# Gates by one ScalarE instruction: Silu for the pool, conv and LayerNorm gates, Tanh with the addition in the eviction for the attention and merge gates

## The chip, the cores and the metric

One core of a Trainium2 chip runs the whole program. The metric is the device time of one execution in microseconds (us), where less is better. The kernel before took 921.75 us in the median of three runs (921.71, 921.75 and 926.39). The profiled execution, from which all rows here come, took 925.56 us. Names in rows: PE is the matmul engine and PEld its weight loads, DVE is VectorE, ACT is ScalarE, POOL is GpSimd, SP is SyncE. "L790" is line 790 of the kernel.

## The reference, cut to what matters

One layer of a hybrid decoder: 1024 prompt tokens and 64 sample tokens (8 sequences of 8) of width 1024, all in fp32. `W` is 512.

```python
h = rmsnorm(x, g_pre)
proj = h @ w_in                                   # 1024 x (7*512 + 3*1024)
p_in, p_gate, c_val, c_glu, c_gate, q, x_gate = [proj[..., i * W:(i + 1) * W] for i in range(7)]
merge_logits = proj[..., 7 * W:].reshape(B, S, 3, D_MODEL)
a = pool_mix(pool_ext, pos0, pool_w, pool_scale) * jax.nn.silu(p_gate)
u = c_val * jax.nn.sigmoid(c_glu)
cv = jax.nn.silu(layernorm(causal_dwconv(conv_ext, conv_w, conv_b), conv_ln_g, conv_ln_b))
bconv = cv * jax.nn.silu(c_gate)
...                                               # o: 4-head attention of q into 256 memory rows
cattn = o * jax.nn.silu(x_gate)
br = jnp.einsum('bsnw,nwd->bsnd', jnp.stack([a, bconv, cattn], axis=2), w_branch)
merged = jnp.sum(jax.nn.sigmoid(merge_logits) * br, axis=2)
x_new = x + rmsnorm(merged @ w_out, g_post)
```

So there are three families of Silu gates on the projections (`p_gate`, `c_gate`, `x_gate`), one Silu after the LayerNorm ("swish"), one sigmoid on `c_glu`, and three sigmoid gates of width 1024 at the merge.

## The kernel before, in words

**Layout.** Tensors lie with channels on the 128 partitions and tokens along the free dimension: 1024 prompt tokens in two halves of 512 (`HALF`), then 64 sample tokens, 1088 in all (`T`). A channel block is a tile `q` of 128x1088 fp32.

**Products.** An fp32 operand is split into two fp16 parts by `hilo`: ACT writes the rounded value (L75), and the rest is written by a subtraction. With a scale of 1.0 that is a TENSOR_TENSOR (L77), on DVE, or on POOL if the caller says so; with any other scale it is a SCALAR_TENSOR_TENSOR on DVE (L79), whatever the caller says. Three matmuls (`mm3`, L85, L88, L89) make one product.

**`pair`.** The input projection goes by pairs of 128-column blocks of `w_in`. One pair is a Strassen-like scheme of 7 products, called stages. Weights come by SP's queue into `raw` tiles; ACT negates some (L498); four DMAs that add at the destination, all issued by POOL (L499, L505, L506, L507), make the sums of weight blocks; `hilo` splits each into a `ws` tile (L75 and L79). ACT (L513) and DVE (L466, `post`) evict the PSUM tiles `pm`: three of the four output blocks of 128x512 end in SBUF, and the fourth, (1, 0), is handed to the caller in PSUM. The caller gives a function `block` for the four blocks and `smp` for the 128x64 sample columns.

**The gates.** `sig_pair` applies a sigmoid to each block (`logistic`, L658): ACT's Sigmoid (L664), or, where `near_exp` is set, ACT's Tanh (L661) and a DVE TENSOR_SCALAR (L662) that makes 0.5*t + 0.5 of it; Tanh is used where the neighbours are exponentials. `silu_pair` (L772) does the same and then multiplies by the projection itself: on POOL for the three blocks that are in SBUF (L790), on DVE from PSUM for block (1, 0) (L788) and the samples (L795). It is called for the attention gate (with `near_exp`), the pool gate and the conv gate (without). The LayerNorm swish takes ACT's Sigmoid (L1093), a DVE TENSOR_SCALAR (L1094) and a POOL multiplication (L1095).

**Attention.** `head` (from L835) multiplies the attention's output in PSUM by the gate tile (L867), splits it and so makes the input `X[2]` of merge 2. The softmax is L824, L827 (Exp), L829 and L832.

**`merge`.** For each of the three branches, eight blocks of gates by `sig_pair`, and for each block the branch projection in three pieces of tokens (364, 364, 360 columns in PSUM tiles `pb`). `ev` (L1155) multiplies piece and gate in one SCALAR_TENSOR_TENSOR, and a DMA issued by POOL (L1161) or DVE (L1157) adds the branches into `M`.

**Out projection.** `pair_of` does `M @ w_out` by the same scheme with M as the stationary side: POOL makes sums of blocks of M into `sr` tiles (L594), `spl` splits them by `hilo` with scale 1.0, and `samples_split` does so for the 64 sample columns, with the subtraction on POOL. DMAs issued by POOL (L1217, `wo_add`) make the sums of `w_out`'s blocks, which are split into `BO`.

**Order.** The sections run in the order conv_pair(0), attn_pair(0), attn_pair(2), conv_pair(2) with the samples' attention, merge(2), pool_pair(0), pool_pair(2), merge(0), cgate_pair(0), cgate_pair(2), merge(1), out projection. A planner hands out stages with side work between: the 120 conv taps of L715 (128x1024 on DVE each) at rates by section, and jobs (softmax, pool mixing, LayerNorm). A scheduler then orders each engine's instructions by a model of their times; the taps are pinned. Every engine runs its list strictly in order, and tiles come from rings of fixed size.

## Time and profile before

| | |
|---|---|
| median of three runs | 921.75 us |
| profiled execution | 925.56 us |
| its span, first to last instruction | 923.8 us |
| mean granted TensorE clock | 0.965 |
| busy: PE, DVE, ACT, POOL | 859.6, 715.1, 465.2, 360.3 us |
| share of the span: PE, DVE, ACT, POOL | 93%, 77%, 50%, 39% |

Times in rows are us unless marked ns. A row of the timeline has start, duration, engine, line, operation, output and input tile, the number of instructions joined, and in brackets how long the engine had stood idle and whose result ended that. A row of a group has the count, the busy time and the mean ns of one, and after the second bar the idle time ahead of them. A row of the table by stages has the stretch, its length, busy time and instruction count of PE, PEld, DVE, ACT and POOL, the granted clock, the DMA share and GB/s.

### The profile page before, as it was taken

How to read it: one execution, taken by the hardware profiler on the slowest of the kernel's cores; microseconds unless marked ns; L12 is line 12 of the kernel's file. 1: busy time of each engine (PE TensorE's matmuls, PEld its weight loads, DVE VectorE, ACT ScalarE, POOL GpSimd, SP SyncE). 2: the span in 40 equal slices, each digit the busy share in tenths (PEclk: the TensorE clock that was granted, in tenths of full speed). 3: DMA queues.
4: the chain of work that ended last, by engine and by line, in shares of the span. 5: the costliest groups of instructions: out<-in, count | busy, mean ns of one | idle time of the engine just before them, and what ended most of it. 6: DMA issues, size and time to landing. Idle time of an engine off the chain costs nothing.

```text
span 923.8 us, 15244 instructions
## 1 busy us (share of the span) xinstructions
PE 859.6 (93%) x5765; PEld 461.0 (50%) x5765; DVE 715.1 (77%) x1119; ACT 465.2 (50%) x990; POOL 360.3 (39%) x392
## 2 busy tenths in 40 slices
PE   5879999999999889999998989999999999988986
PEld 3325455554555545555444445565545555545432
DVE  4697599999967699999988978458565544678876
ACT  8766547554753733323444544356345434745541
POOL 1354152444343361311443775525355212366500
PEclk8869999999999899999999999999999999998998
DMA  8634742424466224334444336444654658472132
GB/s 300 158 65 144 210 97 56 82 68 113 106 224 176 92 39 102 82 80 92 93 95 92 80 86 123 113 110 97 139 117 105 138 122 251 101 158 60 69 126 91
DMA packets 101541, 107.43 MB, mean 116 GB/s; under 512 B 5486, under 2 KB 72036, under 8 KB 101452
## 3 DMA queue, kind: packets, MB, share of 16 engines
q1 hardware_dynamic: 82748, 68.24, 23.5%
q0 software_dynamic: 18720, 38.22, 23.1%
q8 instruction: 45, 0.74, 0.3%
q14 instruction: 28, 0.23, 0.1%
HBM read 62.37 MB, written 6.33 MB: 74 GB/s over the span
## 4 chain that ended last, share of the span: by engine, by line
PE 37%; DVE 15%; issue 5%; ACT 3%; POOL 3%; DMA 3%; DVEq 0%; ACTq 0%; POOLq 0%
PE pm L85 8%; PE pm L89 8%; PE pm L88 8%; DVE q L715 6%; PE pb L85 4%; PE pb L89 4%; PE pb L88 4%; DVE ws L79 3%; DMA raw<-raw 2%; DVE ws L77 1%; POOL sr L594 1%; ACT ws L75 1%; DVE q L1272 1%; DVE q L1265 1%; DVE q L1155 1%
## 5 line engine op out<-in xcount | busy, mean ns | idle before, releaser
L85 PE MATMUL pm<-BO,ws 128*128 128x512 f16 x836 | 319.9, 385 | 17.8 <-ACT h L513 3.7
L89 PE MATMUL pm<-BO,ws 128*128 128x512 f16 x836 | 320.8, 384 | 3.1 <-DVE ws L77 2.8
L88 PE MATMUL pm<-BO,ws 128*128 128x512 f16 x836 | 321.1, 384 | 1.1 <-DVE BO L77 0.6
L79 DVE SCALAR_TENSOR_TENSOR ws<-raw,ws 128x512 f16<-128x512 f32 x228 | 192.9, 863 | 61.2 <-ACT ws L75 59.5
L88 PEld LDWEIGHTS <-ws 128*128 128x128 f16 x1548 | 149.1, 99 | 134.8 <-issue 27.7
L89 PEld LDWEIGHTS <-ws 128*128 128x128 f16 x1548 | 149.3, 99 | 125.0 <-issue 8.0
L85 PEld LDWEIGHTS <-ws 128*128 128x128 f16 x1548 | 148.7, 99 | 117.7 <-issue 9.5
L75 ACT ACTIVATE ws<-raw 128x512 f16<-128x512 f32 x228 | 138.1, 627 | 119.5 <-PE pm L89 57.0
L715 DVE SCALAR_TENSOR_TENSOR q<-q,cw,q 128x1024 f32<-128x1024 f32 x120 | 166.9, 1399 | 4.3 <-ACT q L712 4.0
L85 PE MATMUL pb<-q,ws 128*128 128x364 f16 (+1 forms) x288 | 92.2, 323 | 2.1 <-DVE q L1155 2.1
L89 PE MATMUL pb<-q,ws 128*128 128x364 f16 (+1 forms) x288 | 93.0, 323 | 0.0
L88 PE MATMUL pb<-q,ws 128*128 128x364 f16 (+1 forms) x288 | 92.9, 323 | 0.0
L499 POOL DMA_DIRECT2D raw<-raw x25 | 21.8, 872 | 150.3 <-ACT raw L498 134.1
L513 ACT ACTIVATE h<-pm 128x512 f32<-128x512 f32 x75 | 44.0, 588 | 50.8 <-PE pm L89 47.2
L1155 DVE SCALAR_TENSOR_TENSOR q<-pb,q 128x364 f32<-128x364 f32 (+1 forms) x72 | 37.1, 528 | 30.0 <-PE pb L89 24.4
L466 DVE SCALAR_TENSOR_TENSOR q<-pm,h 128x512 f32<-128x512 f32 x51 | 34.9, 684 | 21.3 <-PE pm L89 13.3
L507 POOL DMA_DIRECT2D raw<-raw x25 | 22.1, 885 | 68.5 <-issue 24.3
L75 ACT ACTIVATE q<-q 128x1024 f16<-128x1024 f32 (+2 forms) x37 | 35.5, 971 | 26.5 <-DVE q L867 12.6
L506 POOL DMA_DIRECT2D raw<-raw x25 | 21.6, 864 | 64.6 <-DVE ws L79 24.7
L498 ACT ACTIVATE raw<-raw 128x512 f32<-128x512 f32 x50 | 31.0, 626 | 30.7 <-DVE ws L79 29.9
L85 PE MATMUL pm<-BS,ws 128*128 128x64 f16 x416 | 43.3, 193 | 1.2 <-DVE q L466 1.2
L664 ACT ACTIVATE q<-q 128x512 f32<-128x512 f32 x36 | 22.6, 627 | 41.7 <-DVE q L466 41.2
(245 smaller groups left out, 1335.1 us busy)
## 6 DMA issues: line engine op xcount, KB each, us to landing
raw<-in_w_in SPq DMA_DIRECT2D x104, 256.0 KB, 2.9
raw<-raw POOLq DMA_DIRECT2D x104, 256.0 KB, 3.2
q<-in_x_prompt SPq DMA_DIRECT2D x16, 512.0 KB, 9.1
q<-q POOLq DMA_DIRECT2D x14, 544.0 KB, 5.5
raw<-in_w_branch SPq DMA_DIRECT2D x24, 256.0 KB, 3.9
q<-in_w_mem_kv SPq DMA_DIRECT2D x8, 512.0 KB, 6.7
q<-in_cache_mem_k SPq DMA_DIRECT2D x8, 512.0 KB, 3.4
q<-in_cache_mem_v SPq DMA_DIRECT2D x8, 512.0 KB, 7.3
```

What stands on the lines that cost most here:

```text
L75: nc.scalar.activation(hi, src, AF.Copy, scale=scale)
L79: nc.vector.scalar_tensor_tensor(lo, src, scale, hi, ALU.mult, ALU.subtract)
L85: ins = nc.tensor.matmul(out, wh, xh, start=start and j == 0, stop=False, skip_group_check=partial)
L88: nc.tensor.matmul(out, wh, xl, start=False, stop=False, skip_group_check=partial)
L89: nc.tensor.matmul(out, wl, xh, start=False, stop=stop and j == n - 1, skip_group_check=partial)
L466: nc.vector.scalar_tensor_tensor(dst, ps, sc, base, ALU.mult, ALU.add)
L498: nc.scalar.activation(A(1, kh), A(1, kh), AF.Copy, scale=-1.0)
L507: nc.gpsimd.dma_start(out=A(0, 1), in_=A(0, 0), accum_op=ALU.add)
L513: nc.scalar.activation(v[name], ps, AF.Copy, scale=sc)
L664: nc.scalar.activation(dst, src, AF.Sigmoid, scale=scale)
L715: ins = nc.vector.scalar_tensor_tensor(acc, src, wj, acc, ALU.mult, ALU.add)
L1155: nc.vector.scalar_tensor_tensor(g, p, 1.0 / WS, g, ALU.mult, ALU.mult)
```

## The change

It replaces four ways of making a gate.

- Pool and conv gates: one ACT instruction, Silu, in place of Sigmoid and a product.
- Attention gate: Tanh of half the argument on ACT, then one DVE SCALAR_TENSOR_TENSOR `(t + 1) * x`. The tile then holds the gate without its factor, which is kept under the key "unit" (0.5, or 0.5/16 for the block out of PSUM), and `head` puts it in.
- LayerNorm swish: one ACT Silu with the LayerNorm's gain and bias as scale and bias.
- Merge gates: Tanh of half the argument in place of Sigmoid, and the eviction computes `(g + 1) * p` in place of `(p / 16) * g`. `M` so holds 32 times its value, and its splits take the factor `MS = 0.5 / WS`: they no longer have the scale 1.0, and the subtraction becomes a SCALAR_TENSOR_TENSOR on DVE, for the samples' columns too, where it was on POOL.

`logistic` stays for conv_pair(2) alone, whose gate keeps Tanh and the TENSOR_SCALAR.

```diff
@@ spl, in pair_of
-                hilo(y, w[:, 0, k], w[:, 1, k])
+                hilo(y, w[:, 0, k], w[:, 1, k], MS)
@@
-    def logistic(dst, src, scale, near_exp):
-        if near_exp:
-            nc.scalar.activation(dst, src, AF.Tanh, scale=0.5 * scale)
-            nc.vector.tensor_scalar(dst, dst, 0.5, 0.5, ALU.mult, ALU.add)
-        else:
-            nc.scalar.activation(dst, src, AF.Sigmoid, scale=scale)
+    def half_tanh(dst, src, scale):
+        nc.scalar.activation(dst, src, AF.Tanh, scale=0.5 * scale)
+    def logistic(dst, src, scale):
+        half_tanh(dst, src, scale)
+        nc.vector.tensor_scalar(dst, dst, 0.5, 0.5, ALU.mult, ALU.add)
...
@@ silu_pair
+        def gate(d, ap, scale):
+            if near_exp:
+                half_tanh(d, ap, scale)
+                nc.vector.scalar_tensor_tensor(d, d, 1.0, ap, ALU.add, ALU.mult)
+            else:
+                nc.scalar.activation(d, ap, AF.Silu, scale=scale)
         def block(r, t0, ap, scale):
-            d = tile_of(r)[:, t0 : t0 + HALF]
-            logistic(d, ap, scale or 1.0, near_exp)
-            if scale:
-                nc.vector.scalar_tensor_tensor(d, ap, scale, d, ALU.mult, ALU.mult)
-            else:
-                nc.gpsimd.tensor_tensor(d, ap, d, ALU.mult)
+            tiles["unit", r, t0] = 0.5 * (scale or 1.0)
+            gate(tile_of(r)[:, t0 : t0 + HALF], ap, scale or 1.0)
         def smp(r, ap):
-            d = tile_of(r)[:, S:]
-            logistic(d, ap, 1.0 / WS, near_exp)
-            nc.vector.scalar_tensor_tensor(d, ap, 1.0 / WS, d, ALU.mult, ALU.mult)
+            gate(tile_of(r)[:, S:], ap, 1.0 / WS)
@@ head
-            nc.vector.tensor_tensor(xg, p, xg, ALU.mult)
+            nc.vector.scalar_tensor_tensor(xg, p, sx["unit", h % 2, tg * HALF], xg, ALU.mult, ALU.mult)
@@ layer_norm
-                sg = half()
-                nc.scalar.activation(sg[:, :n], yb, AF.Sigmoid, scale=ln_g[:, ch : ch + 1], bias=ln_b[:, ch : ch + 1])
-                nc.vector.tensor_scalar(yb, yb, ln_g[:, ch : ch + 1], ln_b[:, ch : ch + 1], ALU.mult, ALU.add)
-                nc.gpsimd.tensor_tensor(yb, yb, sg[:, :n], ALU.mult)
+                nc.scalar.activation(yb, yb, AF.Silu, scale=ln_g[:, ch : ch + 1], bias=ln_b[:, ch : ch + 1])
@@ merge
-    M = [None] * KT
+    M, MS = [None] * KT, 0.5 / WS
-            sig_pair(GATE0 + bi * D + dp * 2 * P, sg)
+            sig_pair(GATE0 + bi * D + dp * 2 * P, sg, half_tanh)
-                    nc.vector.scalar_tensor_tensor(g, p, 1.0 / WS, g, ALU.mult, ALU.mult)
+                    nc.vector.scalar_tensor_tensor(g, g, 1.0, p, ALU.add, ALU.mult)
@@ samples_split
-            hilo(M[k][:, S:], w[:, 0, k], w[:, 1, k], eng=nc.gpsimd)
+            hilo(M[k][:, S:], w[:, 0, k], w[:, 1, k], MS)
```

Three places show how each engine's list changes. Numbers of tiles and lines shift by a few from one kernel to the other.

POOL at the second pool pair before: between the DMAs of the weight sums (L499 to L507) stand three gate products (L790), and a windowed sum of the pool mixing (L990).

```order
181 L499 DMA raw_5493<-raw_5490 128x512
182 L790 TENSOR_TENSOR q_5341<-h_5339,q_5341 128x512
183 L790 TENSOR_TENSOR q_5361<-h_5359,q_5361 128x512
184 L505 DMA raw_5490<-raw_5490 128x512
185 L790 TENSOR_TENSOR q_5341<-h_5449,q_5341 128x512
186 L506 DMA raw_5490<-raw_5493 128x512
187 L990 TENSOR_TENSOR q_5486<-q_5134 128x1038
188 L507 DMA raw_5493<-raw_5490 128x512
```

POOL at the same place after (L993 is the windowed sum):

```order
171 L499 DMA raw_5469<-raw_5466 128x512
172 L505 DMA raw_5466<-raw_5466 128x512
173 L506 DMA raw_5466<-raw_5469 128x512
174 L993 TENSOR_TENSOR q_5462<-q_5116 128x1038
175 L507 DMA raw_5469<-raw_5466 128x512
```

The three products are gone, and the DMAs follow one another; the other rows keep their order.

ACT around the samples' softmax, at the start of merge 2, before: Exp (L827), the split of its result and, between them, table loads for each change from Sigmoid to Exp and back. L712 writes the first tap of a conv channel.

```order
317 L827 ACT_TABLE_LOAD
318 L827 ACTIVATE h_3252,t_3255<-pb_3076,t_3253 128x256
319 L498 ACTIVATE raw_3653<-raw_3653 128x512
320 L834 ACTIVATE h_3252<-h_3252,t_3257 128x256
321 L75 ACTIVATE h_3263<-pb_3260 128x256
322 L513 ACTIVATE h_3287<-pm_3036 128x512
323 L75 ACTIVATE q_3318<-q_3266 128x1024
324 L664 ACT_TABLE_LOAD
325 L664 ACTIVATE q_3289<-q_3289 128x512
326 L75 ACTIVATE q_3421<-q_3316 128x1024
327 L75 ACTIVATE q_3448<-q_3419 128x1024
328 L712 ACTIVATE q_3713<-q_2809,parT,cw 128x1024
```

ACT at the same place after (L660 is the Tanh of a merge gate):

```order
316 L829 ACTIVATE h_3240,t_3243<-pb_3064,t_3241 128x256
317 L498 ACTIVATE raw_3641<-raw_3641 128x512
318 L836 ACTIVATE h_3240<-h_3240,t_3245 128x256
319 L75 ACTIVATE h_3251<-pb_3248 128x256
320 L513 ACTIVATE h_3275<-pm_3024 128x512
321 L75 ACTIVATE q_3306<-q_3254 128x1024
322 L660 ACTIVATE q_3277<-q_3277 128x512
323 L75 ACTIVATE q_3409<-q_3304 128x1024
324 L75 ACTIVATE q_3436<-q_3407 128x1024
325 L712 ACTIVATE q_3701<-q_2797,parT,cw 128x1024
```

The table loads are gone, and the rest stands as it stood. Over the whole list ACT has 11 table loads before and 9 after: three around this softmax go, and one comes, at the first Silu of the pool gates.

POOL as the out projection sets in, before: the DMAs that add blocks of `w_out` (L1217), with six splits of sample columns between them (L77).

```order
294 L1217 DMA raw_8132<-q_8056 128x512
295 L1217 DMA raw_8162<-q_8072 128x512
296 L77 TENSOR_TENSOR ws_8612<-q_3237,ws_8612 128x64
297 L77 TENSOR_TENSOR ws_8612<-q_3289,ws_8612 128x64
298 L77 TENSOR_TENSOR ws_8612<-q_3716,ws_8612 128x64
299 L77 TENSOR_TENSOR ws_8612<-q_3740,ws_8612 128x64
300 L77 TENSOR_TENSOR ws_8612<-q_4018,ws_8612 128x64
301 L77 TENSOR_TENSOR ws_8612<-q_4039,ws_8612 128x64
302 L1217 DMA raw_8178<-q_8091 128x512
303 L1217 DMA q_8056<-raw_8132 128x512
```

POOL at the same place after:

```order
263 L1217 DMA raw_8060<-q_7984 128x512
264 L1217 DMA raw_8090<-q_8000 128x512
265 L1217 DMA raw_8106<-q_8019 128x512
266 L1217 DMA q_7984<-raw_8060 128x512
267 L1217 DMA raw_8060<-raw_8060 128x512
```

The splits have left POOL for DVE (L79), and the DMAs stand next to each other.

More of the change, by code (lines that the diff above doesn't have):

```diff
@@ L656, in hybrid_layer_kernel, with sig_pair @@
     U, Y = [None] * WT, [None] * WT
-    def logistic(dst, src, scale, near_exp):
-        if near_exp:
-            nc.scalar.activation(dst, src, AF.Tanh, scale=0.5 * scale)
-            nc.vector.tensor_scalar(dst, dst, 0.5, 0.5, ALU.mult, ALU.add)
-        else:
-            nc.scalar.activation(dst, src, AF.Sigmoid, scale=scale)
-    def sig_pair(c0, tiles, near_exp=False):
+    def half_tanh(dst, src, scale):
[3 more added lines that the diff above has]
+        nc.vector.tensor_scalar(dst, dst, 0.5, 0.5, ALU.mult, ALU.add)
+    def sig_pair(c0, tiles, fn):
         def tile_of(r):
@@ L676, in block @@
         def block(r, t0, ap, scale):
-            logistic(dest(r, t0), ap, scale or 1.0, near_exp)
+            fn(dest(r, t0), ap, scale or 1.0)
         def smp(r, ap):
-            logistic(tile_of(r)[:, S:], ap, 1.0 / WS, near_exp)
+            fn(tile_of(r)[:, S:], ap, 1.0 / WS)
         pair(c0, dest, block, smp)
@@ L757, in conv_pair @@
             sg = {}
-            sig_pair(3 * W + ch0 * P, sg, True)
+            sig_pair(3 * W + ch0 * P, sg, logistic)
         else:
@@ L954, in sample_attention @@
             kr = vr
-        nc.vector.tensor_tensor(sxs, oS[:, : H * NS].rearrange("p (h t) -> p h t", h=H), sxs, ALU.mult)
+        nc.vector.scalar_tensor_tensor(
+            sxs, oS[:, : H * NS].rearrange("p (h t) -> p h t", h=H), 0.5 / WS, sxs, ALU.mult, ALU.mult)
         for h in range(H):
```

## The prediction

> **What bounds the kernel now.** I read the busy times of the engines first (PE is busy 93% of the span), then the table of busy time by stage, cut where the sections change.
>
> ```profile
> 161.00:235.00 74.00, 69.27 (x452) 38.06 (x450) 71.42 (x113) 41.84 (x102) 32.20 (x31) 1.00 0.40 93
> ...
> 299.00:345.00 46.00, 39.66 (x353) 22.88 (x352) 37.43 (x40) 23.85 (x44) 22.82 (x11) 0.89 0.22 61
> 345.00:437.00 92.00, 91.31 (x585) 49.66 (x582) 91.91 (x106) 34.33 (x66) 17.08 (x17) 1.00 0.40 89
> 437.00:552.00 115.00, 104.61 (x695) 52.10 (x694) 100.78 (x118) 53.26 (x103) 60.25 (x51) 0.99 0.39 92
> 552.00:805.00 253.00, 252.65 (x1710) 138.21 (x1709) 148.99 (x237) 121.54 (x236) 102.59 (x99) 1.00 0.57 129
> 805.00:851.00 46.00, 39.77 (x386) 23.24 (x385) 35.72 (x79) 23.66 (x77) 26.48 (x44) 0.89 0.51 110
> ```
>
> The columns after the length are busy PE, PEld, DVE, ACT and POOL. From 552 to 805 us (merges 0 and 1, the swish, the conv gates) PE idles 253.00 - 252.65 = 0.35 us: no matmul goes away in this change, so whatever it saves on DVE and POOL there is worth nothing. What can be won is PE idle time elsewhere: 4.7 us (attention), 6.3 (samples' softmax, start of merge 2), 10.4 (pool pairs) and 6.2 (start of the out projection). From 345 to 437 DVE is as full as PE, 91.91 of 92, with conv taps. So I looked next for the waits of PE in those stages, each followed back in the timeline to what was late, and asked whether the change takes that away. This is the group of POOL products that goes, and the ACT instructions ahead of it:
>
> ```profile
> L790 POOL TENSOR_TENSOR q<-h,q 128x512 f32<-128x512 f32 x18 | 29.1, 1617 | 16.1 <-ACT q L664 10.6 <-DVE q L662 5.5
> ...
> L664 ACT ACTIVATE q<-h 128x512 f32<-128x512 f32 x12 | 7.4, 621 | 3.2 <-DVE h L466 3.2
> ...
> L661 ACT ACTIVATE q<-h 128x512 f32<-128x512 f32 x6 | 3.8, 632 | 11.3 <-DVE h L466 11.3
> ```
>
> The 18 products of L790 are three in each of six pairs: two each of attention, pool and conv gates. Silu is not in the trace; its nearest rows are Sigmoid (L664) and Tanh (L661) on tiles of its size, 621 and 632 ns, so I cost it as the Sigmoid whose place it takes. Were it twice that, ACT, at some half of its time in every stage above, would still have room.
>
> **Term 1, attention gates.** At 171 to 176 us the softmax of attn_pair(0) meets the gates:
>
> ```profile
> 171.41 0.41 DVE L662 TENSOR_SCALAR q<-q 128x512 f32<-128x512 f32 x1
> ...
> 171.91 2.84 POOL L790 TENSOR_TENSOR q<-h,q 128x512 f32<-128x512 f32 x1 [5.54 <-DVE q L662]
> ...
> 174.21 1.85 DVE L832 TENSOR_SCALAR q<-q,t 128x256 f32<-128x256 f32 x2
> ```
>
> ```profile
> L832 DVE TENSOR_SCALAR q<-q,t 128x256 f32<-128x256 f32 x32 | 11.8, 411 | 0.1
> ```
>
> ```profile
> PE pb L855 <- DVE q L832: 2.3, 3, 0.8
> ```
>
> Two of L832 take 0.8 in the mean over the kernel; this pair took 1.85, with L790 running to 174.75 and POOL's next split behind it. PE waits for L832 three times, 2.3 us in all and 0.8 at most; two of these waits, some 1.5 together, follow this pair. POOL's split moves up to where L790 stood and may collide with other DVE work, so I take half: **-0.8**, bounds 0 and -1.5.
>
> The same in attn_pair(2), at 220 to 226 us. To see here is what DVE's split takes beside POOL, and what PE waits for.
>
> ```profile
> 220.52 1.53 POOL L77 TENSOR_TENSOR q<-q,q 128x512 f16<-128x512 f32 x1
> ...
> 220.84 2.99 DVE L79 SCALAR_TENSOR_TENSOR ws<-raw,ws 128x512 f16<-128x512 f32 x1
> ...
> 221.76 1.51 POOL L790 TENSOR_TENSOR q<-h,q 128x512 f32<-128x512 f32 x1
> ...
> 224.95 0.68 DVE L788 SCALAR_TENSOR_TENSOR q<-pm,q 128x512 f32<-128x512 f32 x1
> ...
> 225.68 0.38 PE L85 MATMUL pm<-BO,ws 128*128 128x512 f16 x1 [1.89 <-DVE q L788]
> ```
>
> An instruction of this size takes 0.68 on DVE (L788), and the split took 2.99 while POOL had two products. It ends at 223.83, 0.56 after L790's end at 223.27; without L790 it would end 0.56 after L77's 222.05, so 1.22 us earlier. L788 stands behind it, one tap later, and PE waits 1.89 for the PSUM tile that L788 frees. The change also takes the TENSOR_SCALAR (0.41 above) out of DVE's queue between split and eviction. Both together are 1.5 us of the 1.89; bounds 0 and -1.9. Term: **-1.5**.
>
> What the new instruction costs: a TENSOR_SCALAR of 0.41 is replaced by a SCALAR_TENSOR_TENSOR of 0.68, +0.27 for each of six blocks (+1.6), while block (1, 0), twice, falls from 0.41 + 0.68 to 0.68 (-0.8) and the samples lose their TENSOR_SCALAR. DVE's own work so stays about as it is, and I cost it at nothing; if the contention did not go, the 0.27 in front of each eviction would be PE's, 1.6 at most. In `head`, TENSOR_TENSOR becomes SCALAR_TENSOR_TENSOR with the same two tensors; rows of the two kinds of equal size stand under the third rival: nothing.
>
> The Trainium skill, "VectorE: DVE Perf Modes", section "The perf-mode tier table", speaks against this swap: an fp32 instruction with one source in SBUF runs at twice the rate of one with two tensors. The trace agrees in direction, 0.41 against 0.68. By the rule alone, without the contention, the attention gates would be 0.8 us slower on DVE instead of 2.3 faster on PE, and the sum below 3.1 smaller.
>
> **Term 2, table loads.** Three loads of 1.28 us around the samples' softmax go; one comes at the first pool gate, where ACT has 53.26 busy of 115, and I cost it at nothing. The three are seen to matter at one place:
>
> ```profile
> 316.88 1.28 ACT L664 ACT_TABLE_LOAD   x1
> ...
> 321.99 1.24 ACT L712 ACTIVATE q<-q,parT,cw 128x1024 f32<-128x1024 f32 x1 [1.29 <-POOL q L77]
> ...
> 323.27 4.94 DVE L715 SCALAR_TENSOR_TENSOR q<-q,cw,q 128x1024 f32<-128x1024 f32 x2 [4.04 <-ACT q L712]
> ```
>
> DVE stood idle 4.04 us for L712, which stood behind a POOL split, behind ACT's split, behind the load. Earlier by up to 1.28, the taps bring forward the evictions behind them in DVE's list, for which PE waits as part of this stage's 6.3 us. The load before Exp gains nothing: the reciprocal behind Exp sits in DVE's list behind a pinned tap. Half of the load: **-0.7**, bounds 0 and -1.3.
>
> **Term 3, pool gates.** First pair, at 480 to 492 us:
>
> ```profile
> 480.94 1.59 POOL L790 TENSOR_TENSOR q<-h,q 128x512 f32<-128x512 f32 x1
> ...
> 482.56 1.10 DVE L1011 SCALAR_TENSOR_TENSOR q<-pb,psc,q 128x364 f32<-128x364 f32 x2 [2.92 <-POOL q L790]
> ```
>
> ```profile
> 491.62 0.62 PE L85 MATMUL pb<-q,pws 128*128 128x364 f16 x3 [2.11 <-ACT q L75]
> ```
>
> DVE idles 2.92 for L790, the last product of the gate tile into which L1011 multiplies the mixed pool. Silu ends where the Sigmoid ended, ahead of the product; L1011 could follow at once, and the work behind it reaches the split for which PE waits 2.11. The wait is shorter than DVE's, and POOL's windowed sum comes earlier too, beside DVE's work, so not all of it goes: **-1.6**, bounds 0 and -2.1.
>
> Second pair, at 521 to 543 us, the dearest wait that the change touches:
>
> ```profile
> 521.89 3.02 POOL L790 TENSOR_TENSOR q<-h,q 128x512 f32<-128x512 f32 x2
> ...
> 524.86 0.84 POOL L505 DMA_DIRECT2D raw<-raw  x1
> ...
> 529.91 0.87 POOL L506 DMA_DIRECT2D raw<-raw  x1 [2.90 <-DMA raw<-raw]
> ...
> 534.17 1.15 ACT L75 ACTIVATE ws<-raw 128x512 f16<-128x512 f32 x2 [2.16 <-DMA raw<-raw]
> ...
> 538.65 0.47 PE L85 MATMUL pm<-BO,ws 128*128 128x512 f16 x1 [3.21 <-DVE q L466]
> ...
> 542.27 0.38 PE L85 MATMUL pm<-BO,ws 128*128 128x512 f16 x1
> ...
> 542.71 0.38 PE L89 MATMUL pm<-BO,ws 128*128 128x512 f16 x1
> ```
>
> Two products stand ahead of the DMA L505, whose landing releases L506, whose landing releases ACT's and DVE's splits, whose DVE time sets the eviction L466. Without the products L505 starts near 521.9, 2.95 us earlier, and the chain of DMAs moves with it: of the 3.21 us wait 2.9 go. Behind the wait PE runs slow: nine matmuls from 538.65 to 542.27 are 0.40 apart, afterwards 0.22, so 9 x 0.18 = 1.6 us more. Waits of 1.89 and 2.11 above were followed by no such spell; if 0.3 is left, it goes too. Together **-4.5**, bounds 0 (something else on POOL or DVE holds the eviction) and -4.8.
>
> The Trainium skill, "TensorE: Matmul & The Clock Gate", section "What's actually happening", has the clock halve after an idle window of about 3.4 us that runs freely. Here a wait of 3.21 was enough. Taking the rule as strict, the slow spell would have another cause and stay, and the term would be -2.9.
>
> **Term 4, out projection.** POOL loses the samples' splits that stand among its DMAs:
>
> ```profile
> 815.37 2.52 POOL L77 TENSOR_TENSOR ws<-q,ws 128x64 f16<-128x64 f32 x6
> ...
> 831.49 4.65 DVE L79 SCALAR_TENSOR_TENSOR BO<-q,BO 128x512 f16<-128x512 f32 x1 [0.57 <-ACT BO L75]
> ```
>
> ```profile
> 825.71 0.59 PE L85 MATMUL pm<-BO,ws 128*128 128x512 f16 x1 [2.50 <-ACT h L632]
> ...
> 837.45 0.61 PE L89 MATMUL pm<-BO,ws 128*128 128x512 f16 x1 [2.83 <-DVE ws L77]
> ```
>
> The first wait is for an eviction that ACT issued behind a split of a landed DMA, so issuing later DMAs up to 2.5 us earlier could end it; the second lies behind DVE's split of 4.65 us beside POOL's sums. But the twelve DMAs share the same DMA engines, and an earlier one only makes the next land later. All 5.3 us and some of the slow clock (0.89) gone would be -7; DVE takes over eight splits of about 0.21, +1.7, at most 1 of it ahead of a wait. I take **-1.5**, near the low end, because the trace shows DMAs and not their issue behind the first wait; bounds +1 and -7.
>
> **At nothing:** the merge gates (Tanh for Sigmoid on ACT; the eviction still one SCALAR_TENSOR_TENSOR from PSUM), the swish and the conv gates (under PE's full 253 us, with DVE at 149 and POOL at 103; they would cost only if ACT, at 122, came to hold PE), and the splits of M with a factor (rows under the third rival).
>
> **Sum:** -1.5 - 0.8 - 0.7 - 1.6 - 4.5 - 1.5 = -10.6 us. Against the profiled execution's 925.56 (span 923.8, 1.8 around it) that is 915.0. The median of the runs shown is 921.75, 3.8 below the profiled one, and the waits should be the same in it: 921.75 - 10.6 = 911.1.
>
> **Rivals.** *All waits go, the tail's too* (-1.9 - 1.5 - 1.3 - 2.1 - 4.8 - 7 = -18.6): 903. For it: each has L790 or L77 of POOL close ahead. Against it: in the tail twelve DMAs wait for each other.
>
> *The time is given back:* terms 1 and 2 fall in a stretch that ends in 345 to 437, where DVE has no slack and its pinned taps must all be done, and term 3's chain through two DMAs is held by the next thing. Then only about a quarter remains: 921.75 - 2.7 = 919. For it: 91.91 busy of 92. Against: term 3, over half of the sum, lies behind that stretch.
>
> *Slower, by the splits of M in the out projection.* All 112 splits of 128x128 become two-tensor instructions with a scalar, on the DVE queue that PE waits for at 837.
>
> ```profile
> L77 DVE TENSOR_TENSOR ws<-sr,ws 128x128 f16<-128x128 f32 x64 | 19.1, 344 | 3.3 <-ACT ws L75 3.2
> ...
> L79 DVE SCALAR_TENSOR_TENSOR BO<-q,BO 128x512 f16<-128x512 f32 x20 | 22.0, 1111 | 2.9 <-ACT BO L75 2.9
> ```
>
> ```profile
> L77 DVE TENSOR_TENSOR q<-esn,q 128x64 f16<-128x64 f32 x4 | 0.9, 215 | 0.0
> ...
> L79 DVE SCALAR_TENSOR_TENSOR q<-pm,q 128x64 f16<-128x64 f32 x4 | 0.8, 212 | 0.0
> ```
>
> Equal sizes cost the same, 212 and 215. But L79 in the out projection averages 1111 against 0.68 us undisturbed, a factor of 1.6 beside POOL. If the new form suffers by that factor where the old did not, 112 x 0.344 x 0.6 = 23 us come onto DVE. It decides if more than 15.3 of them reach the end (10.6 saved, 4.6 to be slower): about 935 at the full 23. Against it: the old form reads the same two tensors, and 344 beside POOL's sums already holds its share.
>
> *The change is undone by tables:* had Silu needed a load at each turn to Tanh, it would cost 1.28 each; the list of instructions has 9 loads for 11, so this is out.
>
> **How the numbers follow.** Under 0.5% (4.6 us) a measurement of this kernel can't tell from no change, its own runs lying 0.5% apart. Faster then ends at 917.1, slower begins at 926.4. My forecast (905 to 917): 0.64; all waits go, about 903: 0.12; given back, 917 to 923: 0.17; slower by the splits: 0.07. The first two make faster 0.76. The range takes in the forecast's bounds and most of the neighbouring rivals: 902 to 920; about the forecast alone, 905 to 917.
>
> **What would show it.** PE's waits for L788 at 223, L832 at 174, for ACT's split at 489 and L466 at 535 are gone or under 0.5 us, the stage 437 to 552 shrinks by some 6 us and the length of the PE-full stretch of 253 stays. Wrong would be: the wait at 535 still over 2 us with another releaser, DVE idle less but PE's waits unchanged, L79 in place of L77 over 400 ns for 128x128, or a tail longer than before.

## The result, and the profile after

The changed kernel took 915.84 us (median of seven runs, 913.09 to 919.26), the kernel before 925.26 (median of seven, 921.71 to 926.39): a ratio of 0.991, 95% interval 0.989 to 0.994, or some 8 us less (5.9 to 10.2). Measured again on another chip, the ratio was 0.991 (0.988 to 0.994). The forecast was 911.1, range 902 to 920, from a sum of -10.6 us. The profiled execution of the changed kernel has a span of 913.7 us, against 923.8. Its table by stage, cut where the prediction's was:

```profile
161.00:235.00 74.00, 71.84 (x476) 39.75 (x474) 73.03 (x119) 45.24 (x112) 26.97 (x26) 1.00 0.39 89
...
299.00:345.00 46.00, 39.56 (x352) 22.20 (x351) 38.16 (x41) 22.38 (x47) 23.66 (x12) 0.93 0.26 67
345.00:437.00 92.00, 89.83 (x594) 49.11 (x592) 92.00 (x106) 32.37 (x61) 14.79 (x16) 1.00 0.40 89
437.00:552.00 115.00, 107.14 (x686) 53.46 (x686) 92.78 (x110) 55.05 (x104) 53.87 (x49) 0.99 0.41 91
552.00:805.00 253.00, 253.00 (x1711) 138.37 (x1710) 133.08 (x222) 122.69 (x243) 77.00 (x78) 1.00 0.57 128
805.00:851.00 46.00, 40.29 (x380) 22.63 (x379) 40.49 (x94) 25.51 (x85) 30.11 (x50) 0.89 0.51 110
```

DVE lost 16 us and POOL 26 in the stretch from 552 to 805, and PE is as full as before: nothing was won there. Between 437 and 552 PE idles 7.9 us in place of 10.4, where the forecast had some 6 less.

Cuts at fixed times mix work that has moved. PE's own work marks the same place in every kernel: ahead of its matmuls 526, 831, 1392, 2900, 4211, 5114 and 5700 (of 5765, counted from 0) the same matmuls have run in all fourteen profiles, and the time between two marks is a stage's length. An instruction of another engine is no such mark: the ACT eviction L513 at the end of merge 2 stands 14 matmuls, some 3 us of PE's work, earlier in the kernels with the new attention gates than in the others. From the timelines, in us (columns: head, up to the first gates of attention, attention, samples' softmax and merge 2, pool gates and the start of merge 0, merges 0 and 1, out projection, end):

```
kernel      head  -att   att  merge2  pool  merges  out   end
before     118.5  45.6  89.2  211.3  206.6  134.9   94.7  23.1
b_again    115.1  48.6  88.1  210.9  208.3  134.9   95.5  23.1
changed    114.8  48.8  85.7  211.1  203.9  134.9   91.9  22.6
a_again    115.3  45.6  84.5  212.6  204.9  134.9   92.0  22.6
u_att      115.0  45.6  87.9  210.4  202.8  135.1   91.6  22.6
u_pool     115.1  48.8  85.5  211.2  206.2  134.9   92.0  22.6
u_pool1    116.1  47.2  84.5  211.1  206.6  134.9   92.9  22.6
u_pool2    115.5  46.3  85.7  211.7  207.4  135.1   92.6  22.6
u_split    115.4  49.9  85.2  211.5  204.7  134.9   94.9  22.6
u_smp      117.2  50.3  84.1  212.4  204.0  134.9   92.4  22.6
u_tab      115.8  48.8  84.5  212.7  204.0  135.1   92.2  22.6
u_ln       116.8  47.1  85.5  211.2  206.9  135.3   91.3  22.6
nq21       116.1  50.2  84.1  212.4  206.9  136.4   91.6  22.6
late4      114.8  45.6  84.5  211.0  203.6  134.9   95.1  22.6
```

No edit touches head and -att, and they still differ by 4 and 5 us from one execution to the next. In the later columns a stage that no edit touched agrees mostly within 1.6 us, but not always: late4's out projection takes 95.1 where nine others of the same code take 91.3 to 92.9. So one profile by itself doesn't show an effect of under some 3 us, and the times of whole kernels, with intervals of 0.2 to 0.3% to each side (2 to 3 us), hardly do either.

**Attention.** The waits of PE for the softmax's scaling at 174 us and for L788 at 223 us are gone. The new instructions by form, Silu on ACT and Tanh's addition and product on DVE (L788 is this product now, not the one of before):

```profile
L790 ACT ACTIVATE q<-h 128x512 f32<-128x512 f32 x12 | 7.4, 624 | 1.3 <-DVE h L466 1.2
...
L788 DVE SCALAR_TENSOR_TENSOR q<-q,h 128x512 f32<-128x512 f32 x6 | 4.8, 798 | 0.0
```

Silu costs 624 ns where the Sigmoid cost 621. With two operands in SBUF DVE takes 0.68 us in five of the six and 1.38 in the sixth, 798 ns in the mean, so the forecast's 0.68 held.

**Pool.** POOL, DVE and PE at the second pair after the change, from the timeline:

```profile
514.99 0.88 POOL L499 DMA_DIRECT2D raw<-raw  x1 [2.85 <-ACT raw L498]
...
518.46 0.86 POOL L505 DMA_DIRECT2D raw<-raw  x1 [2.58 <-DMA raw<-raw]
...
522.67 0.86 POOL L506 DMA_DIRECT2D raw<-raw  x1 [3.35 <-DMA raw<-raw]
...
527.85 0.88 POOL L507 DMA_DIRECT2D raw<-raw  x1 [2.37 <-issue]
528.46 6.96 POOL L993 TENSOR_TENSOR q<-q 128x1036 f32<-128x1036 f32 x3
...
530.71 0.69 DVE L466 SCALAR_TENSOR_TENSOR q<-pm,h 128x512 f32<-128x512 f32 x1 [4.67 <-POOL q L993]
...
531.45 0.38 PE L85 MATMUL pm<-BO,ws 128*128 128x512 f16 x1 [2.01 <-DVE q L466]
```

Rows of before that belong to the first of these and to the eviction:

```profile
521.04 0.87 POOL L499 DMA_DIRECT2D raw<-raw  x1
...
534.83 3.16 DVE L79 SCALAR_TENSOR_TENSOR ws<-raw,ws 128x512 f16<-128x512 f32 x2 [1.40 <-ACT ws L75]
```

Before, L505 began 3.82 us after L499 (521.04 to 524.86) with two products between them; now it begins 3.47 after, with nothing between: POOL waits 2.58 us for L499 to land, 3.2 us after it began. The whole chain from L499 to L507 takes 12.9 us (13.4 in a second profile) in place of 13.6. PE still waits 2.01 for the eviction L466, which is now late for another reason: before, it stood behind two splits that ended at 537.99; now DVE idles 4.67 for POOL's windowed sum L993, behind L507. Then PE waits 0.43 and 1.27 more within 12 us.

**First pool pair.** A tap now stands ahead of an eviction and of the split for which PE waits (DVE, then PE):

```profile
461.55 1.28 DVE L715 SCALAR_TENSOR_TENSOR q<-q,cw,q 128x1024 f32<-128x1024 f32 x1
462.75 0.69 DVE L466 SCALAR_TENSOR_TENSOR h<-pm,h 128x512 f32<-128x512 f32 x1
463.35 1.22 DVE L77 TENSOR_TENSOR q<-q,q 128x1024 f16<-128x1024 f32 x1
```

```profile
462.24 0.31 PE L85 MATMUL pb<-q,pws 128*128 128x364 f16 x1 [1.25 <-ACT q L75]
464.62 0.46 PE L88 MATMUL pb<-q,pws 128*128 128x364 f16 x1 [2.07 <-DVE q L77]
...
466.99 0.63 PE L85 MATMUL pm<-BO,ws 128*128 128x512 f16 x1
```

Ten matmuls behind the second wait run slow (those of 512 columns take 0.63 us in place of 0.38). Before, the waits were shorter, and no slow matmuls followed them:

```profile
466.27 0.32 PE L85 MATMUL pb<-q,pws 128*128 128x364 f16 x1 [1.13 <-ACT q L75]
467.53 0.31 PE L88 MATMUL pb<-q,pws 128*128 128x364 f16 x1 [0.94 <-DVE q L77]
```

### The profile page after: what moved, and what is told of

Same layout as the page of the kernel before. It is cut to its first block, busy times and chain, and to the rows that moved or that the text cites. A ratio compares the mean times of both kernels' runs of the same rounds, so it can differ in the third digit from the quotient of the medians.

```text
span 913.7 us, 15151 instructions
## 1 busy us (share of the span) xinstructions
PE 852.5 (93%) x5765; PEld 458.3 (50%) x5765; DVE 693.6 (76%) x1097; ACT 462.1 (51%) x988; POOL 319.7 (35%) x354
## 5 line engine op out<-in xcount | busy, mean ns | idle before, releaser
L85 PE MATMUL pm<-BO,ws 128*128 128x512 f16 x836 | 317.8, 382 | 10.2 <-ACT h L513 3.2
L79 DVE SCALAR_TENSOR_TENSOR ws<-raw,ws 128x512 f16<-128x512 f32 x228 | 188.0, 841 | 73.7 <-ACT ws L75 71.9
L85 PE MATMUL pb<-q,ws 128*128 128x364 f16 (+1 forms) x288 | 92.4, 322 | 2.0 <-DVE q L1155 2.0
L499 POOL DMA_DIRECT2D raw<-raw x25 | 21.9, 877 | 198.3 <-ACT raw L498 182.5
L513 ACT ACTIVATE h<-pm 128x512 f32<-128x512 f32 x75 | 44.2, 591 | 49.4 <-PE pm L89 49.3
L1155 DVE SCALAR_TENSOR_TENSOR q<-q,pb 128x364 f32<-128x364 f32 (+1 forms) x72 | 37.3, 526 | 32.7 <-PE pb L89 27.8
L466 DVE SCALAR_TENSOR_TENSOR q<-pm,h 128x512 f32<-128x512 f32 x51 | 34.9, 685 | 29.8 <-PE pm L89 12.8
L77 POOL TENSOR_TENSOR q<-q,q 128x1024 f16<-128x1024 f32 (+1 forms) x17 | 36.8, 2175 | 25.8 <-ACT q L75 25.8
L507 POOL DMA_DIRECT2D raw<-raw x25 | 22.0, 882 | 66.6 <-DVE ws L79 22.1
```

The costliest lines, as they stand in the source:

```text
L77: (eng or nc.vector).tensor_tensor(lo, src, hi, ALU.subtract)
L79: nc.vector.scalar_tensor_tensor(lo, src, scale, hi, ALU.mult, ALU.subtract)
L85: ins = nc.tensor.matmul(out, wh, xh, start=start and j == 0, stop=False, skip_group_check=partial)
L466: nc.vector.scalar_tensor_tensor(dst, ps, sc, base, ALU.mult, ALU.add)
L507: nc.gpsimd.dma_start(out=A(0, 1), in_=A(0, 0), accum_op=ALU.add)
L513: nc.scalar.activation(v[name], ps, AF.Copy, scale=sc)
```

## The experiments

Theory A was the prediction's sum with its four terms. Theory B, formed from the two traces, had the same total from other sizes: more from attention and the out projection, and the pool gates' gain cut short because the queue of DMAs waits for landings, not for POOL. A rival to both was that the head of the kernel (some 3 us ahead in the changed kernel's profile at 118 us) was part of the gain. Times are medians of the kernel against before on the same chip; ratios have their 95% interval.

### Before and after once more (b_again, a_again)

No edit in either.

> The kernel before once more, unchanged, for a second profile. In the first, the stretch up to 118 us, where both kernels have the same instructions in the same order, took 3.0 us longer than in the changed kernel's. If that is chance, this profile is ahead of the first one by 1 to 3 us at 118 us, and the 3 us wait for DVE's split at 132 us can appear here too, since it would come from PE being early there. If it is a property of the kernel, this profile equals the first within 0.5 us up to 118 us. The second pool pair: the DMA L505 starts 3.8 us after L499 as in the first, and the slow spell behind PE's wait at 535 us comes back if it belongs to that wait.

> The changed kernel once more, unchanged, on the chip of the other runs of this call, as the common measure for them: ratio to before between 0.989 and 0.994, some 916 us. Its profile: the wait of 3 us at 132 us is there or not, by chance; the waits of 2.1 us at the first and 2.0 us at the second pool pair are there again.

Measured: b_again 923.02 us, ratio 1.000 (0.998 to 1.002); a_again 914.32, 0.991 (0.988 to 0.994). The head of b_again is 3.4 us shorter than in the first profile, so the lead there is chance: PE idles 22 us in both, but 25 in place of 41 matmuls run slow. In b_again and the changed kernel the lead is lost at a split that takes 4.35 us beside POOL's work. The rows are of b_again (first) and of the changed kernel (the others):

```profile
135.40 0.28 PE L89 MATMUL pb<-q,q 128*128 128x256 f16 x1 [2.85 <-DVE q L79]
```

```profile
128.95 4.35 DVE L79 SCALAR_TENSOR_TENSOR ws<-raw,ws 128x512 f16<-128x512 f32 x1
...
129.16 2.46 POOL L77 TENSOR_TENSOR q<-q,q 128x1024 f16<-128x1024 f32 x1
...
135.28 0.28 PE L89 MATMUL pb<-q,q 128*128 128x256 f16 x1 [3.04 <-DVE q L79]
```

This wait stands in b_again, the changed kernel and four of its variants (u_pool, u_split, u_smp, nq21) and is missing in the other eight profiles, where the same split takes 0.7 to 1.8 us: not a trace of the change. Nor does an early start bring it, as the expectation had it: a_again, u_att and late4 have as short a head without it, u_smp has it with a head of 117.2. The second pool pair of before repeats: L505 3.8 us after L499, PE's wait of 3.19 and twelve slow matmuls behind it. So do the changed kernel's waits: 2.06 at the first pair in a_again, and 2.64 at the second, longer than the 2.0 expected.

### Attention gates put back (u_att)

```diff
-                half_tanh(d, ap, scale)
-                nc.vector.scalar_tensor_tensor(d, d, 1.0, ap, ALU.add, ALU.mult)
+                logistic(d, ap, scale)      # then, as before, the product: DVE if in PSUM, else POOL
+                ...                         # head's factors "unit" and 0.5 / WS become 1.0
```

> The changed kernel with the attention gates alone put back: Tanh, the TENSOR_SCALAR on DVE and the product on POOL, and the TENSOR_SCALAR's result used in head with factor 1. If the prediction's term 1 is right, 2.3 us of the gain go, so about 2.3 us slower than the changed kernel (some 918), and the waits of PE for the softmax's scaling and for the eviction out of PSUM come back (1.5 and 1.9 us). If the 3 us wait that the changed kernel's trace shows at 132 us is caused by the new gates, it is gone here and the two nearly cancel: within 1 us of the changed kernel. If that wait is chance, it can be there or not.

Measured: 915.77 us, 0.993 (0.991 to 0.996). The stage of attention is 87.9 us, as before the change (89.2 and 88.1), where the eleven kernels with the new gates have 84.1 to 85.7, 84.9 in the mean. PE's waits come back at both places:

```profile
172.40 0.33 PE L867 MATMUL pb<-ident,q 128*128 128x128 f32 x1 [0.83 <-DVE q L844]
...
220.97 0.38 PE L85 MATMUL pm<-BO,ws 128*128 128x512 f16 x1 [1.85 <-DVE q L798]
```

So term 1 is right in its mechanism, and 3.0 us in this profile instead of 2.3. Yet the whole kernel is not clearly slower, since the stages behind it are shorter: merge 2 takes 210.4 where the kernels with the new attention gates and without the table loads take 211.6 in the mean, and the pool stage 202.8 in place of 203.9 to 204.9 where attention has the new gates and nothing in the stage is edited. With the old attention gates the tap does not stand ahead of the eviction, PE's waits at 461 us are 1.13 and 0.94 again, though ten matmuls behind them run slow, and those at 485 to 498 us of before do not come back.

### Pool and conv gates put back (u_pool), and each pool pair alone (u_pool1, u_pool2)

```diff
-                nc.scalar.activation(d, ap, AF.Silu, scale=scale)
+                nc.scalar.activation(d, ap, AF.Sigmoid, scale=scale)
+                ...    # then the product: DVE if ap is in PSUM, else POOL; for all, the first or the second pool pair
```

> The changed kernel with the pool and conv gates alone put back: Sigmoid, products on POOL for three blocks and on DVE for the fourth and the samples. Theory A, the prediction's term 3: 6.1 us slower than the changed kernel (some 922), with a PE wait of 3 us at the second pool pair. Theory B, from the changed kernel's trace: the DMA L505 there waits 2.6 us for the landing of the DMA L499 ahead of it, so the products of POOL stood in a time in which the queue had to wait for that DMA anyway: L505 starts 3.5 us after L499 in the one and 3.8 in the other, and undoing it costs 1 to 3 us (917 to 919), most of it at the first pool pair, where PE's wait of 2.1 comes back.

> The changed kernel with the gates of the second pool pair alone put back (Sigmoid, three products on POOL, one on DVE, and one more table load). The list puts two of the products ahead of the DMA L499 and one between L505 and L506. The prediction's step for this place: 4.5 us slower, PE waiting over 3 us for the eviction L466 there, with a slow spell behind it. Theory B, the DMAs' landings set the pace of that queue and POOL has time for the products between them: PE's waits at that place change by less than 1 us in sum, and the time stays within 1.5 us of the changed kernel.

> The changed kernel with the gates of the first pool pair alone put back (three products on POOL, one of them between L507 and the windowed sums; one more table load). The prediction's step: 1.6 us slower at 480 to 500 us, with DVE's wait of 2.9 us for the product and PE's of 2.1 us for ACT's split. If undoing the pairs adds up (the second alone moved the profile by 3.4 us, both with the conv gates by 2.4), this one alone moves it by under 1 us or makes it faster; if they do not add, because the waits of the second pair are set by the chain that comes out of the first, it is again 1.5 to 3 us slower by itself.

Measured: u_pool 919.69 us, 0.996 (0.994 to 0.998); u_pool2 918.84, 0.996 (0.994 to 0.999); u_pool1 917.73, 0.994 (0.992 to 0.996). The pool stage is 206.2, 207.4 and 206.6, against 204.3 in the mean of the five kernels that leave it alone (changed, a_again, u_split, u_smp, u_tab): each is 1.9 to 3.1 longer, both pairs together no more than one alone. So the parts do not add, and the expectation that one pair alone would be free was wrong. But with a pair alone the test itself brings a table load into this stage, and that load is part of what is measured. In u_pool1 PE's one new wait is for the Silu of the second pair, behind the load (ACT, then PE):

```profile
516.28 1.28 ACT L791 ACT_TABLE_LOAD   x1
...
519.00 0.38 PE L85 MATMUL pm<-BO,ws 128*128 128x512 f16 x1 [2.06 <-ACT q L791]
```

In u_pool, which has no additional load there, the wait at the second pair is near what it is in the changed kernel (1.97), with no slow matmuls behind it, against theory A; PE's 2.1 us wait at the first pair did not return, against the place that theory B named. The sizes don't decide: the stage is 1.9 us longer, which fits B (1 to 3 us), while the whole kernel is some 4 us slower by the ratios, between B and A (6.1), with 2 to 3 us of uncertainty. u_pool2, also some 4 us slower, was dearer than theory B allowed and has the long wait and the slow spell of theory A:

```profile
513.29 3.26 POOL L800 TENSOR_TENSOR q<-h,q 128x512 f32<-128x512 f32 x2 [2.13 <-ACT q L796]
516.50 0.86 POOL L499 DMA_DIRECT2D raw<-raw  x1
...
519.96 0.86 POOL L505 DMA_DIRECT2D raw<-raw  x1 [2.59 <-DMA raw<-raw]
```

```profile
533.55 0.58 PE L85 MATMUL pm<-BO,ws 128*128 128x512 f16 x1 [4.40 <-DVE q L466]
533.93 0.63 PE L88 MATMUL pm<-BO,ws 128*128 128x512 f16 x1
```

Products ahead of L499 hold up the whole chain of DMAs, while L505 keeps its 3.46 us behind L499. POOL idled 2.13 for the Sigmoid of these products, which itself stood behind the added load of 1.28. Before the change the products stood behind L499, where the landing hid all but 0.35 us.

### Table loads put back (u_tab)

```diff
-            sig_pair(GATE0 + bi * D + dp * 2 * P, sg, half_tanh)
+            sig_pair(..., half_tanh if bi != 2 else lambda d, x, sc: nc.scalar.activation(d, x, AF.Sigmoid, scale=sc))
```

> The changed kernel, but with Sigmoid in place of Tanh in the gates of merge 2 alone, the evictions as they are (so the values of these gates are others than the reference's): the table loads around the samples' softmax come back, nothing else changes. Prediction's term 2: 0.7 us slower (between 0 and 1.3). The two traces moved by 1.1 to 1.3 us against each other at that place: if that was the loads, 1.3 us slower, with DVE's wait for the first tap of ACT near 4 us in place of the changed kernel's 2.8 or so. If the loads cost nothing, within the uncertainty of the changed kernel and no shift of PE between 310 and 335 us.

Measured: 916.84 us, 0.994 (0.992 to 0.996). DVE's wait for the first tap, in u_tab and in the changed kernel:

```profile
319.16 4.94 DVE L715 SCALAR_TENSOR_TENSOR q<-q,cw,q 128x1024 f32<-128x1024 f32 x2 [4.76 <-ACT q L712]
```

```profile
318.24 4.94 DVE L715 SCALAR_TENSOR_TENSOR q<-q,cw,q 128x1024 f32<-128x1024 f32 x2 [3.66 <-ACT q L712]
```

The wait is 1.1 us longer, but in the eleven profiles without the loads it lies between 3.30 and 5.09, so this doesn't show that the loads did it. The stage takes 212.7 against 211.6 in the mean of the ten kernels with the new attention gates and without the loads (211.0 to 212.6): 1.1 more, in line with a term of 0.7 between 0 and 1.3, and not to be told from the scatter.

### Splits of M put back (u_split), the samples' alone (u_smp)

```diff
-                hilo(y, w[:, 0, k], w[:, 1, k], MS)
+                hilo(y, w[:, 0, k], w[:, 1, k])                        # u_split only
-            hilo(M[k][:, S:], w[:, 0, k], w[:, 1, k], MS)
+            hilo(M[k][:, S:], w[:, 0, k], w[:, 1, k], eng=nc.gpsimd)   # both
```

> The changed kernel with the splits of M alone put back to a scale of 1 (TENSOR_TENSOR on DVE, the samples' on POOL); M keeps its factor of 32, which the last normalization takes out but for its epsilon. Prediction's term 4: 1.5 us slower (some 917), with POOL's six splits of 128x64 again between the first DMAs of the out projection. If the tail's gain of some 2.7 us in the two traces all comes from this, 2.7 us slower. Rival, that the splits as SCALAR_TENSOR_TENSOR cost more on DVE: faster than the changed kernel by over 1 us, and the mean of the 128x128 splits is lower here than there.

> The changed kernel, but the eight splits of M's sample columns alone go back to POOL with a scale of 1 (these columns so keep the factor of 32); all other splits of M as SCALAR_TENSOR_TENSOR with the factor. POOL's list has the six splits between the second and the third DMA of the out projection again. With all splits put back, the stretch from 794 to 900 us was 3.0 us longer in the profile. Theory: all of it is these splits, which hold the DMAs up by 2.5 us: the stretch is 2 to 3.5 us longer than in the changed kernel here too, with PE's waits of 2.5 and 2.8 us in it. Rival, the form of the other 112 splits matters: under 1 us longer here.

Measured: u_split 916.12 us, 0.994 (0.992 to 0.996); u_smp 919.84, 0.995 (0.992 to 0.998). The out projection takes 94.9 in u_split, as before the change (94.7 and 95.5), against 92.0 in the mean of nine kernels that leave it alone (91.3 to 92.9). The exception is late4 with 95.1, where PE waits 3.56 and 2.71 and 22 matmuls run slow against 12 to 20; as it has the new splits, u_split's one profile doesn't prove that the old ones cost 3 us. u_smp has POOL's splits and PE's first wait back:

```profile
812.26 2.53 POOL L77 TENSOR_TENSOR ws<-q,ws 128x64 f16<-128x64 f32 x6
```

```profile
822.54 0.38 PE L85 MATMUL pm<-BO,ws 128*128 128x512 f16 x1 [2.43 <-ACT h L632]
830.83 0.59 PE L85 MATMUL pm<-BO,ws 128*128 128x512 f16 x1 [2.47 <-ACT ws L75]
834.28 0.61 PE L89 MATMUL pm<-BO,ws 128*128 128x512 f16 x1 [2.43 <-DVE ws L79]
```

Yet the stage takes 92.4, 0.4 more than the mean, as the rival had it: the theory of 2 to 3.5 us failed. By the whole kernel u_smp is some 3 us slower than the changed one, with intervals that overlap; this profile does not show where. With the new splits PE waits at this place too. A split of 128x64 takes 0.21 us on DVE for six of the eight, but the seventh, beside POOL's sums, took 3.37 us in the changed kernel and 5.39 in a_again (rows of a_again, DVE and PE):

```profile
820.73 5.39 DVE L79 SCALAR_TENSOR_TENSOR ws<-q,ws 128x64 f16<-128x64 f32 x1
...
826.17 0.21 PE L88 MATMUL pb<-ws,BO 128*128 128x64 f16 x1 [3.97 <-DVE ws L79]
```

What the other 112 splits add in u_split stays open, since their means are nearly equal. The new form in the changed kernel, and the old one in u_split:

```profile
L79 DVE SCALAR_TENSOR_TENSOR ws<-sr,ws 128x128 f16<-128x128 f32 x64 | 20.0, 357 | 2.2 <-ACT ws L75 2.2
```

```profile
L77 DVE TENSOR_TENSOR ws<-sr,ws 128x128 f16<-128x128 f32 x64 | 19.4, 350 | 2.8 <-ACT ws L75 2.7
```

357 against 350 ns: the rival that would have made the kernel slower is out.

### The swish put back (u_ln)

```diff
-                nc.scalar.activation(yb, yb, AF.Silu, scale=ln_g[...], bias=ln_b[...])
+                sg = half()    # Sigmoid into sg, tensor_scalar on DVE, product on POOL, as before
```

> The changed kernel with the swish alone put back (Sigmoid, a TENSOR_SCALAR on DVE, a product on POOL; 12 blocks each, and one more table load). Prediction: nothing, since PE is full from 552 to 805 us; within 1 us of the changed kernel, and PE idle under 0.7 us in that stretch. Rival: the gain that the terms do not explain sits here; 2 us slower or more.

Measured: 918.73 us, 0.995 (0.992 to 0.997), 4.4 us above a_again on the same chip, with intervals that overlap. In the stretch of the swish PE stays full:

```profile
555.00:802.60 247.60, 247.05 (x1676) 135.00 (x1675) 142.47 (x228) 121.64 (x237) 87.51 (x90) 1.00 0.58 131
```

PE idles 0.55 us there, so the expectation for the place holds. The pool stage of this profile is 2.6 longer than the mean; some 1.5 of it arises by 480 us, ahead of the swish, where 16 slow matmuls follow PE's 2 us wait in place of 9 to 11. Whether the swish is worth a further microsecond or two, this run can't say.

### Two tries at the second pool pair (nq21, late4)

```diff
-NQ = 20
+NQ = 21                                                        # nq21: one more 128x1088 buffer
-        if 0 <= s + BASE < n and stages[s + BASE][7]:
+        ...  # late4: the weight sums of merge 0's first gate pair with a lead of 4 stages, all others 8
```

> The changed kernel with 21 instead of 20 buffers in the ring of 128x1088 tiles. In its trace PE waits 2.0 us at the second pool pair for DVE's eviction L466, which stood idle 4.7 us for POOL's windowed sum L993: the eviction needs a buffer that this sum frees, and the sum stands on POOL behind the DMA L507, which waits for L506's landing. If the missing buffer is what holds PE there, the wait goes, 1.5 to 2 us of time. If PE then waits for the same chain of DMAs by way of the splits L79, as before the change, the wait only gets another name and the time stays within 0.7 us.

> The changed kernel, but the weight sums of the first gate pair of merge 0 (L499 to L507 at 515 to 528 us) are handed out four stages later in the program, so that POOL's list has a windowed sum L993 between L505 and L506 and one between L506 and L507, where POOL waits 3.4 and 2.4 us for landings. If PE's waits there (2.0 for the eviction that needs a buffer from L993, 1.3 for the pool mixing's split) hang on the windowed sums standing behind L507, the sums end some 2 us earlier against L507, the waits shrink by 1 to 3 us and the kernel is that much faster than the changed one, some 914. If the later start of the DMA chain only moves the wait to the weights' splits, PE waits as long or longer for an L79 or L75 there and it is the same or up to 3 us slower.

Measured: nq21 919.50 us, 0.996 (0.993 to 0.998), slower than the changed kernel if anything; late4 915.17, 0.992 (0.989 to 0.995), the same. In nq21 the wait at that eviction is gone, and PE, being early, waits longer for the pool mixing:

```profile
545.89 0.82 PE L85 MATMUL pb<-q,pws 128*128 128x364 f16 x3 [4.85 <-ACT q L75]
```

In late4 the windowed sums fill POOL's waits as meant, and the first wait shrinks to 0.23, but the splits of the later weights hold PE next, four of them taking 9.26 us on DVE while POOL works, with slow matmuls behind (DVE, then PE):

```profile
524.47 9.26 DVE L79 SCALAR_TENSOR_TENSOR ws<-raw,ws 128x512 f16<-128x512 f32 x4 [1.45 <-ACT ws L75]
```

```profile
530.15 0.38 PE L85 MATMUL pm<-BO,ws 128*128 128x512 f16 x1 [0.23 <-ACT q L660]
...
534.39 0.38 PE L85 MATMUL pm<-BO,ws 128*128 128x512 f16 x1 [2.36 <-DVE q L466]
```

PE reaches this place ahead of two chains, the four DMAs in a row with their splits and the windowed sums behind them on the same queue, and whichever wait is taken away, the other one follows. No version tried beats the changed kernel.

## Why the prediction was right, and where it was not

Direction and range held. The size was somewhat too large: -10.6 us was forecast, and the ratio of 0.991 gives about -8 (5.9 to 10.2). The time forecast, 911.1, lay 4.7 below the measured 915.84; 3.5 of that is its base, the median of three runs (921.75), where seven runs have 925.26. Differences of the means in the table by stage, from attention on, add up to -9.8, of which 0.4 lies in the end, in no term, and the terms have these parts:

- **Term 1, attention gates, -2.3.** The stage lost 3.7 (88.6 to 84.9), and 3.0 came back in u_att. The mechanism held; the size was too small, because the prediction counted two of PE's three waits for L832 and took half of those. What it left out is what the gates do downstream: in u_att merge 2 and the pool stage together are 2.7 us shorter than the means, so nearly all of the gain is given back there. That a list with fewer DVE instructions gets its pinned taps at other places was in no term.
- **Term 2, table loads, -0.7.** Not seen: the stage takes 211.1 before and 211.6 after. u_att, without the loads but with the old attention gates, has 210.4 and u_tab 212.7, both in line with the term, but neither outside the scatter.
- **Term 3, pool gates, -6.1.** The step that failed. The stage lost 3.1 (207.5 to 204.3), and undoing gives 1.9 to 3.1 back, where a pair alone is undone partly by the test's own table load. The first pair went as forecast at its place (the wait at 491 us is gone; matmuls 3020 to 3225 take 29.8 in place of 34.0), and gave most of it back at 461 us, where the two waits grew by 1.25 us and slow matmuls followed (2900 to 3020 take 23.3 in place of 20.5). At the second pair the prediction let L505 start 2.95 us earlier "without the products". It did not ask what else L505 waits for: L499 reads the block that L505 overwrites, and lands 3.2 us after its start. L505 gained 0.35. The forecast's own sign of error, a wait of 2 us for another reason, is what came (2.01, and 2.64 in a_again).
- **The slow spell of 1.6 us in that term** did go with the wait of 3.2 (none at 2.01 in the changed kernel, nor at 2.64 in a_again), as forecast; u_pool2's 4.40, late4's 2.36 and one of 2.77 in u_split's profile brought it back.
- **Term 4, out projection, -1.5.** The stage lost 3.1 (95.1 to 92.0), within the bounds of +1 and -7, and u_split, in one profile, gives it back. The two waits did not simply go: they were 2.50 and 2.83, and are 2.76 and 1.30 in the changed kernel, 1.23 and 3.97 in a_again. In sum PE idles 8.4 and 9.0 us in the stage in place of 10.0 and 10.2. The eight splits that move to DVE were priced at 1.7 us with at most 1 ahead of a wait; they took 5.1 and 6.9, most of it in the seventh, for which PE waits 3.97 in a_again.
- **At nothing:** the swish, the conv and merge gates changed no PE time in the full stretch: the stage of merges 0 and 1 takes 134.9 before and after.

Too much in terms 2 and 3 (1.2 and 3.0) and too little in terms 1 and 4 (1.4 and 1.6) nearly cancelled; that the sum came near owes something to luck. How much of the pool stage's and the out projection's gain each edit makes is argued from single profiles, and stays open within some 3 us.

On contention, the trace and the Trainium skill's "SBUF — State Buffer" ("Who interferes with whom", and the section on its two sides) agree in kind, that a DVE instruction with two SBUF inputs and a POOL instruction that reads SBUF exclude each other: the split of 4.35 us above, 0.7 to 1.8 in other profiles, stands beside POOL's subtractions. The rule of the Trainium skill's "VectorE: DVE Perf Modes", section "The perf-mode tier table", that an instruction with two tensors is dearer in fp32 than one with one, also held here: the new DVE instruction took 0.68 us in five of six cases, against 0.41 to 0.47 in eleven of twelve of the TENSOR_SCALAR L662 before. It did not decide the stage's length.

## What to carry to other kernels

Before crediting a queue with the time of a removed instruction, list every wait of the next one on that queue, data hazards of DMAs included: an instruction that stood in a DMA's latency was nearly free (here two products cost 0.35 us). Price an instruction moved from POOL to DVE with what POOL does beside it there: here one split of 0.21 us became one of 3.4 to 5.4. Follow the work that PE reaches after a removed wait; where two chains end close together, as at the pool pairs here, the next one takes back most of the gain, and undoing the parts one by one does not add up. Look whether a test that undoes a part brings in something of its own, as the table loads here. Compare the lengths of the same stage in two profiles of each kernel, not start times in one (here 3 us of head were chance), and mark the stages by the bounding engine's own work: an ACT eviction shifted by 14 matmuls against PE.

## What the runs showed that was not expected

- The same waits were followed by slow matmuls in one execution and not in another: those of 1.13 and 0.94 us at 461 us by ten in u_att, by none in before and b_again. Single waits of 2.01, 2.64 (a_again) and 2.65 (u_ln) were followed by none, one of 2.36 (late4), with another of 0.23 four microseconds ahead of it, by eight. So it is not the length of one wait alone that sets the clock. The Trainium skill, "TensorE: Matmul & The Clock Gate", section "What's actually happening", has the clock halve after an idle window of about 3.4 us that runs freely of the kernel. That the same waits count in one execution and not in another agrees with a window that runs freely; that 2.07 us of waits were enough is short of a whole idle window.
- A lead of 3 us by chance in the head was lost 15 us later in some profiles and kept in others: one DVE split took 4.35 us beside POOL in six of fourteen, and 0.7 to 1.8 in the rest.
- Silu needs no more of ACT than Sigmoid (624 against 621 ns), and it shares its table with Tanh, since no load stands at the turns from pool gates to merge gates; Sigmoid beside Silu does need one (10 loads in u_pool1 against 9).
